# Band attention on TensorE: two heads' products with the keys' low parts side by side, on 64 rows of the array each

## The chip, the cores and the metric

The kernel runs on one core of a Trainium2 chip. Its time is device microseconds (us) for one launch; the median of several runs counts. TensorE (PE) multiplies, VectorE (DVE), ScalarE (ACT) and GpSimd (POOL) work on what comes out, SyncE (SP) issues most DMAs. In this program a TensorE product is a weight load of a stationary tile of up to 128 rows by 128 columns, and then the product itself, which streams a moving tile's columns past it.

## The reference, cut to what matters

The whole is one step of a two-layer encoder: an mLSTM layer and an attention layer, each with a squared-ReLU MLP. The change is in the attention layer: 16 query heads, four for each of 4 key heads, 64 numbers a head, chunks of 64 queries, each of which sees its own chunk and the eight before it.

```python
    def one_chunk(args):
        ci, qb = args
        kb = lax.dynamic_slice_in_dim(kp, ci * CHUNK, span, axis=1)
        vb = lax.dynamic_slice_in_dim(vp, ci * CHUNK, span, axis=1)
        s = jnp.einsum('bqkgd,bskd->bkgqs', qb, kb).astype(jnp.float32) * (HD_B ** -0.5) + bias
        valid = (ci * CHUNK - BAND + jnp.arange(span)) >= 0
        s = jnp.where(valid, s, -jnp.inf)
        p = jax.nn.softmax(s, axis=-1).astype(vb.dtype)
        return jnp.einsum('bkgqs,bskd->bqkgd', p, vb)
```

`span` is 576. There are 16 chunks of the prompt, and a sample of 32 queries, which sees 512 cached keys and its own 32.

## The kernel before, in words

**Numbers in two parts.** Queries and keys are held as a high part (rounded to the format fp32r) and a low part (what the rounding left). A query tile has 128 rows: a head has 64 numbers, and its high part lies in one half of the rows, its low part in the other. Which half holds the high part is set by the head (`hd`, L1712). The keys lie twice: `kk[0]` holds the high part in both halves, `kk[1]` the low part in both halves. So one product with `kk[0]` gives (q high + q low) times k high, and one with `kk[1]` gives (q high + q low) times k low; both are summed in PSUM.

**Units and groups.** A unit is 128 query rows: two heads of one chunk. A group (class `Group`, L1869) is one chunk c and one key head, so two units (`pr` 0 and 1). Two groups (e = 0 and 1) make a pair, whose outputs share one PSUM tile. Chunks 8 to 15 have 576 keys ("wide": each product in two parts of 288 columns); chunks 0 to 7 have 64 to 512 ("slim"). The sample is chunk 16, with one unit in a group. The list `todo` (L1917) runs over two halves of the heads (gp); in each it alternates a wide chunk with a slim one or the sample, 17 pairs, 34 groups. The first two groups (chunk 7) are begun in the stage before.

**A group's way.** `softmax_unit` (L1797): TensorE writes the scores into a PSUM tile `s` (L1804; two buffers of two banks). VectorE adds the bias, scales and takes the minimum in one pass (L1814) into `p`; that frees `s`. ScalarE takes the exponential with its sum (L1817). `normalize`: VectorE's reciprocal (L1823), GpSimd's multiply (L1825). `transposed` (L1827): TensorE turns `p` in blocks of 128 (L1839) into PSUM tiles `pt` (three buffers, each holding four blocks: two key blocks of both units), and ScalarE and VectorE in turn copy them to `pT` (L1848, L1850). `weighted_values` (L1854): for each key block TensorE multiplies the values with both groups' `pT`, one group on 64 columns of the array, the other on the other 64 (L1861, fp32, which the trace records as two products each); ScalarE and VectorE write the result's two parts over the queries (L1866, L1867).

**The order.** The loop at L1986 writes TensorE's order by hand. In step n it is: scores of unit 0 of group n; in odd steps the values of the pair before last; the first four transposes of group n-3; scores of unit 1; the remaining transposes. Every engine works through its own list in order. ScalarE's and VectorE's lists are laid out by the framework from this order (ScalarE's by hand in the first steps alone).

Of the kernel before, what the change touches and what calls it, by code (L numbers as in the profile page):

```python
# [75 lines left out]
def trunk_kernel(ctx: ExitStack, tc: tile.TileContext, a, o):  # L76
# [1610 lines left out]
    for gi, grp in enumerate(((0, 1, 2), (3,))):  # L1687
        ws = {pr: [wblock(f"q{pr}_{half}", wq, 512 * half, 256 * pr) for half in range(2)] for pr in grp}
        for ti, (t0, n) in enumerate(TBS):
            if gi == 0:  # L1690
                flow.finish(norms[ti])
                if ti == 1:
                    flow.finish(norms[2])
                    acc_cm0.__exit__(None, None, None)
                qo_cm.append(tc.tile_pool(name=f"qo{ti}", bufs=1, reuse_waits="tile"))
                QOT.append(qo_cm[ti].__enter__().tile([P, 2, 2, 6 if ti < 2 else 5, 256], F32R, name=f"QO{ti}"))
                if ti == 2:
                    nc.vector.memset(qo(16)[:, :, :, 128:256].bitcast(F32), 0.0)
# [95 lines left out]
    nun, near, groups = [7], {}, {}  # L1794
    bank_n[0] += 6

    def softmax_unit(qst, g, k0, nk, bt, off, mx, nm):  # L1797


        s = bank(f"s_{nm}")[:, None] if near else psT.tile([P, 2, 512], F32, tag="s", name=f"s_{nm}", bufs=2)  # L1800
        parts = [(0, 0, nk)] if nk <= 512 else [(0, 0, nk // 2), (1, nk // 2, nk // 2)]
        for b, j0, w in parts:
            for i in range(2):
                nc.tensor.matmul(s[:, b, :w], qst, kk[i][:, g, k0 + j0:k0 + j0 + w], start=(i == 0), stop=(i == 1))  # L1804
# [64 lines left out]
    class Group:  # L1869


        def __init__(self, gp, c, e):
            self.gp, self.c, self.e, self.g = gp, c, e, 2 * gp + e
            self.nm = f"{gp}_{c}"
            self.mx = at.tile([P, 3, 2], F32, tag="mx", name=f"mx_{self.nm}_{e}", bufs=6)
            self.units = []
            self.n = 2 if c < 16 else 1
            if c < 16:
                self.nk, self.k0 = min(c + 1, 9) * 64, max(0, c - 8) * 64
                self.off = self.k0 % P  # L1880
                self.wid, self.vt0 = self.off + self.nk, (self.k0 - self.off) // P
            else:
                self.nk, self.k0, self.off, self.wid, self.vt0 = 544, TP, 0, 544, 8

        def scores(self, pr):
            if pr >= self.n:
                return
            bt = near[self.e][:, pr] if near else \
                bias[2 * self.g + pr][:, 576 - self.nk:] if self.c < 16 else sbias[self.g]
            self.units.append(softmax_unit(qo(self.c)[:, self.e, self.gp, pr * P:(pr + 1) * P], self.g, self.k0, self.nk,  # L1890
                                           bt, self.off, self.mx[:, :, pr], f"{self.nm}_{self.e}{pr}"))
# [275 lines left out]
```

## Time and profile before

| what | value |
|---|---|
| median of 3 runs | 2409.55 us (2406.93 to 2409.78) |
| the profiled execution's own time | 2412.41 us |
| its span, first to last instruction | 2410.6 us |
| TensorE busy in the span | 2342.7 us, 97% |
| the attention loop | about 1412 to 1601 us of the span |
| granted TensorE clock, mean | 0.995 |

A row of the timeline is start, length, engine, line, operation, tile written and read, array used (rows*columns), moved shape and count; rows of equal neighbours are merged, and a row's length reaches to the end of its last one. Results of a product come out some time after its columns have gone in, so the next row can start before a row ends.

### The profile page before, as it was taken

To read this page: it belongs to the slowest core of one execution; us is meant where nothing else is said; L and a number is where in the kernel's file an instruction comes from. 1 tells how busy PE (TensorE), PEld (TensorE's weight loads), DVE (VectorE), ACT (ScalarE), POOL (GpSimd) and SP (SyncE) were. 2 spreads that over 40 slices of the span, in tenths; PEclk is the share of its full clock that TensorE was granted. 3 is DMA by queue.
4 is the path that set the end of the run, shared out by engine and by line. 5 is a ranking of instruction groups with operands and counts; after the bars stand their busy time and mean duration, and the time that the engine had idled before them with its cause. 6 is when DMAs were issued, how large, how long until landed. Compare 5 with 4: busy or idle time off the path is not lost. (4 is left out here: it accounts for less than half of the span.)

```text
span 2410.6 us, 44188 instructions
## 1 busy us (share of the span) xinstructions
PE 2342.7 (97%) x17180; PEld 2250.4 (93%) x17180; DVE 1939.0 (80%) x3903; ACT 1206.0 (50%) x2454; POOL 168.1 (7%) x320
## 2 busy tenths in 40 slices
PE   7999999999999999999999999999999999899997
PEld 4999999999999999999999987789999999899997
DVE  4888766778788789989888777756998889888778
ACT  4565557278666630101147467773776777222212
POOL 0111100000000000000000224420000000000003
PEclk9999999999999999999999999999999999999999
DMA  8343222526566896675512330051486779976642
GB/s 302 120 131 103 78 89 66 177 91 206 184 198 200 279 336 230 252 261 215 183 56 89 82 93 1 10 140 59 165 278 211 259 278 335 355 256 236 224 146 73
DMA packets 284277, 424.64 MB, mean 176 GB/s; under 512 B 15384, under 2 KB 205228, under 8 KB 278948
## 3 DMA queue, kind: packets, MB, share of 16 engines
q1 hardware_dynamic: 279860, 391.48, 48.3%
q10 hardware_dynamic: 4208, 30.35, 3.1%
q8 instruction: 135, 2.21, 0.4%
q14 instruction: 74, 0.61, 0.1%
HBM read 305.96 MB, written 118.17 MB: 176 GB/s over the span
## 5 line engine op out<-in xcount | busy, mean ns | idle before, releaser
L1082 DVE SCALAR_TENSOR_TENSOR ACX<-dn,ada,ACX 128x264 f32<-128x264 f32 (+6 forms) x664 | 281.8, 447 | 83.2 <-PE dn L1452 41.1
L1452 PE MATMUL dn<-fx,wf_d 128*128 128x264 f32 x2016 | 254.1, 285 | 6.8 <-DVE ACX L1082 3.5
L1452 PEld LDWEIGHTS dn<-fx,wf_d 128*128 128x128 f32 x2016 | 248.8, 188 | 9.0 <-DVE ACX L1082 3.0
L89 ACT CAST w_dn<-raw_dn 128x1024 fp32r<-128x1024 f32 x36 | 37.7, 1050 | 282.1 <-DVE aw L279 136.9
L118 PE MATMUL dn<-hs,w_dn 128*128 128x384 f32 (+2 forms) x512 | 161.2, 315 | 0.0
L119 PE MATMUL dn<-hs,w_dn 128*128 128x384 f32 (+2 forms) x512 | 161.0, 315 | 0.0
L120 PE MATMUL dn<-hs,w_dn 128*128 128x384 f32 (+2 forms) x512 | 156.4, 314 | 1.3 <-DVE w_dn L90 1.3
L1317 PE MATMUL up<-TF,wf_u 128*128 128x264 f32 x1056 | 143.2, 285 | 3.8 <-ACT H L1320 3.8
L1317 PE MATMUL up<-U,wf_u 128*128 128x264 f32 x1056 | 140.3, 285 | 1.7 <-ACT H L1320 1.2
L1317 PE MATMUL up<-u,wf_u 128*128 128x264 f32 x1056 | 139.7, 285 | 1.3 <-ACT wf_u L89 0.7
L279 DVE SCALAR_TENSOR_TENSOR aw<-radw,cs,aw 128x512 f32<-128x512 f32 x196 | 139.5, 743 | 1.1 <-DMA radw<-in_w_ada_dram 1.1
L1317 PEld LDWEIGHTS up<-TF,wf_u 128*128 128x128 f32 x1056 | 134.4, 189 | 4.8 <-ACT H L1320 4.6
L1317 PEld LDWEIGHTS up<-U,wf_u 128*128 128x128 f32 x1056 | 133.0, 188 | 3.0 <-ACT H L1320 1.6
L1317 PEld LDWEIGHTS up<-u,wf_u 128*128 128x128 f32 x1056 | 132.9, 188 | 1.9 <-ACT wf_u L89 0.9
L118 PE MATMUL dn<-U,w_dn 128*128 128x384 f32 (+2 forms) x416 | 129.4, 312 | 0.6 <-DVE ada L304 0.6
L119 PE MATMUL dn<-U,w_dn 128*128 128x384 f32 (+2 forms) x416 | 129.4, 312 | 0.0
L120 PE MATMUL dn<-U,w_dn 128*128 128x384 f32 (+2 forms) x416 | 125.9, 313 | 0.6 <-DVE w_dn L90 0.5
L1817 ACT ACTIVATE p<-p,mx 128x576 f32<-128x576 f32 (+9 forms) x132 | 86.6, 657 | 27.5 <-DVE mx L1814 25.2
L120 PEld LDWEIGHTS dn<-hs,w_dn 128*128 128x128 f32 x512 | 96.0, 188 | 2.0 <-DVE w_dn L90 1.8
L118 PEld LDWEIGHTS dn<-hs,w_dn 128*128 128x128 f32 x512 | 96.5, 189 | 0.1
L119 PEld LDWEIGHTS dn<-hs,w_dn 128*128 128x128 f32 x512 | 96.6, 189 | 0.0
L90 DVE TENSOR_TENSOR HL<-H,HL 128x1056 fp32r<-128x1056 f32 x64 | 80.3, 1254 | 20.0 <-ACT HL L89 19.9
(403 smaller groups left out, 7111.0 us busy)
## 6 DMA issues: line engine op xcount, KB each, us to landing
hpl<-HL SPq DMA_DIRECT2D x144, 264.0 KB
rdn_u<-in_w_up_dram SPq DMA_DIRECT2D x64, 512.0 KB
hd<-HL SPq DMA_DIRECT2D x28, 1056.0 KB
fx<-hd SPq DMA_DIRECT2D x50, 528.0 KB
radw<-in_w_ada_dram SPq DMA_DIRECT2D x24, 1024.0 KB
hd<-HM SPq DMA_DIRECT2D x28, 792.0 KB
raw_up<-in_w_up_dram SPq DMA_DIRECT2D x40, 512.0 KB
raw_dn<-in_w_down_dram SPq DMA_DIRECT2D x36, 512.0 KB
```

The source lines that it names most:

```text
L89: nc.scalar.copy(dst_h, src)
L90: (eng or nc.vector).tensor_sub(dst_l, src, dst_h.bitcast(F32))
L118: nc.tensor.matmul(ps, wh, mov(0, k), start=(k == 0), stop=False)
L119: nc.tensor.matmul(ps, wh, mov(1, k), start=False, stop=False)
L120: nc.tensor.matmul(ps, wl, mov(0, k), start=False, stop=(k == nk - 1))
L279: nc.vector.scalar_tensor_tensor(acc[cnd], raw[:, k], sc, acc[cnd], op0=ALU.mult, op1=ALU.add)
L1082: nc.vector.scalar_tensor_tensor(xs, ps[:, off + o:off + o + mm_], gate[:, fc, cnd:cnd + 1], xs, op0=ALU.mult, op1=ALU.add)
L1317: nc.tensor.matmul(p, self.ws[w][:, wl, k], moving(f, tp, xl, k), start=first and k + n_ == 0, stop=k == 3 and n_ == 2, skip_group_check=n ...
L1452: nc.tensor.matmul(p, ws[w][:, wl, k], t[:, s0, xl], start=first and k + n_ == 0, stop=k == kg - 1 and n_ == 2, skip_group_check=not first)
L1817: nc.scalar.activation(z, z, AF.Exp, bias=mx[:, 0:1], scale=-1.0, accum_out=mx[:, 1:2])
```

## The change

The scores of a group are no longer taken unit by unit. `high` takes unit 0 with the keys' high parts; `low` takes unit 1 with the high parts, and then both units with the low parts: each product reads only the 64 rows that hold that unit's high query part, rows 0 to 63 for unit 0 and 64 to 127 for unit 1, and the two are issued one behind the other. The product of the two low parts is dropped there. So that the high query part lies in the right half, L1712 chooses the half by unit instead of by head. The sample and the first two groups keep full products.

```diff
-                        hi, lo = dst[64 * hd:64 * hd + 64], dst[64 - 64 * hd:128 - 64 * hd]
+                        h0 = 0 if cnd else 64 * (fc % 2)
+                        hi, lo = dst[h0:h0 + 64], dst[64 - h0:128 - h0]
...
+        def key_products(self, pr, i, rows=slice(0, P)):
+
+            if pr == len(self.ss):
+                self.ss.append(score_tile(f"{self.nm}_{self.e}{pr}"))
+            for b, j0, w in key_parts(self.nk):
+                nc.tensor.matmul(self.ss[pr][:, b, :w], qo(self.c)[rows, self.e, self.gp, pr * P:(pr + 1) * P],
+                                 kk[i][rows, self.g, self.k0 + j0:self.k0 + j0 + w], start=(i == 0), stop=(i == 1))
+
+        def high(self):
+            self.key_products(0, 0)
+
+        def low(self):
...
+            if self.n == 1 or near:
+                for pr in range(self.n):
+                    if pr:
+                        self.key_products(pr, 0)
+                    self.key_products(pr, 1)
+                return
+            self.key_products(1, 0)
+            for b, j0, w in key_parts(self.nk):
+                for pr in range(2):
+                    r = slice(64 * pr, 64 * pr + 64)
+                    nc.tensor.matmul(self.ss[pr][:, b, :w], qo(self.c)[r, self.e, self.gp, pr * P:(pr + 1) * P],
+                                     kk[1][r, self.g, self.k0 + j0:self.k0 + j0 + w], start=False, stop=True)
```

The loop's order changes with it. The reductions of both units (`scores`) are now issued behind `low`. In odd steps the order is values, `high`, `low`, all transposes; in even steps four transposes, `high`, the other transposes, `low`.

```diff
-            if new is not None:
+            if n == 4:
                 groups[n] = Group(*todo[n][:3])
-                groups[n].scores(0)
-            if n == 4:
+                groups[n].high()
                 groups[1].values()
             if done and done.e and n > 5:
                 done.values()
...
             turn = old.turn() if old else iter(())
-            next(turn, None)
+            if n % 2 == 0 and n > 5:
+                next(turn, None)
             if new is not None:
-                groups[n].scores(1)
+                if n != 4:
+                    groups[n] = Group(*todo[n][:3])
+                    groups[n].high()
+                if n % 2 == 0 or n < 6:
+                    for _ in turn:
+                        pass
+                groups[n].low()
+                for pr in range(2):
+                    groups[n].scores(pr)
             for _ in turn:
                 pass
```

What that does to TensorE's list, in the first half of the heads, in the step that scores chunk 4 for e = 0 and then takes the values of chunk 5. A name is tile_half_chunk_group-and-unit: `s_0_4_01` is the scores of chunk 4, group e = 0, unit 1; `k0` and `k1` are the keys' high and low parts. Before:

```order
L1804 MATMUL s_0_4_01_16036<-k0_14692,QO0_13787 128x320
L1804 MATMUL s_0_4_01_16036<-k1_14693,QO0_13787 128x320
L1839 MATMUL pt_0_5_1_2_16042<-ident_64,p_0_5_10_15898 128x128
L1839 MATMUL pt_0_5_1_2_16042<-ident_64,p_0_5_11_15925 128x128
L1804 MATMUL s_0_4_10_16047<-k0_14692,QO0_13787 128x320
L1804 MATMUL s_0_4_10_16047<-k1_14693,QO0_13787 128x320
L1861 MATMUL pv_0_5_16053<-pT_0_5_0_16000,V_14694 64x256
L1861 MATMUL pv_0_5_16053<-pT_0_5_1_16029,V_14694 64x256
```

Of the change:

```order
L1892 MATMUL s_0_4_00_16030<-k0_14692,QO0_13787 128x320
L1841 MATMUL pt_0_5_1_2_16032<-ident_64,p_0_5_10_15915 128x128
L1841 MATMUL pt_0_5_1_2_16032<-ident_64,p_0_5_11_15918 128x128
L1892 MATMUL s_0_4_01_16036<-k0_14692,QO0_13787 128x320
L1912 MATMUL s_0_4_00_16030<-k1_14693,QO0_13787 128x320
L1912 MATMUL s_0_4_01_16036<-k1_14693,QO0_13787 128x320
L1863 MATMUL pv_0_5_16046<-pT_0_5_0_16008,V_14694 64x256
L1863 MATMUL pv_0_5_16046<-pT_0_5_1_16022,V_14694 64x256
```

Unit 0's scores were done before the step's last transposes and are now finished by the first of the two 64-row products (L1912); the values follow the 64-row products directly, without the next group's unit 0 between them.

And ScalarE's list around the exponentials of chunk 14, group e = 1 (`p_14_10` and `p_14_11`, units 0 and 1), while chunk 5 is turned (`pT_5_0` and `pT_5_1`, its two groups). Before:

```order
L1817 ACTIVATE p_14_10_15981,mx_14_1_15975<-p_14_10_15981,mx_14_1_15975 128x576
L1866 CAST QO_14296<-pv_13_15984 128x256
L1848 COPY pT_5_0_16000<-pt_5_0_0_16001 128x512
L1817 ACTIVATE p_14_11_16012,mx_14_1_15975<-p_14_11_16012,mx_14_1_15975 128x576
L1848 COPY pT_5_1_16029<-pt_5_1_0_16030 128x512
```

Of the change:

```order
L1868 CAST QO_14296<-pv_13_15975 128x256
L1850 COPY pT_5_0_16008<-pt_5_0_0_16009 128x512
L1819 ACTIVATE p_14_10_16002,mx_14_1_15991<-p_14_10_16002,mx_14_1_15991 128x576
L1819 ACTIVATE p_14_11_16005,mx_14_1_15991<-p_14_11_16005,mx_14_1_15991 128x576
L1850 COPY pT_5_1_16022<-pt_5_1_0_16023 128x512
```

The exponential of unit 0 moved from ahead of the write-out of the values of chunk 13 to behind the copy of `pt_5_0_0`; both exponentials now stand between the two copies.

More of the change, by code (lines that the diff above doesn't have):

```diff
@@ L1795, in trunk_kernel, with key_parts, score_tile, softmax_unit @@
     bank_n[0] += 6
[L1797 to L1804, printed above, removed]
+    def key_parts(nk):
+        return [(0, 0, nk)] if nk <= 512 else [(0, 0, nk // 2), (1, nk // 2, nk // 2)]
+    def score_tile(nm):
+        return bank(f"s_{nm}")[:, None] if near else psT.tile([P, 2, 512], F32, tag="s", name=f"s_{nm}", bufs=2)
+    def softmax_unit(s, nk, bt, off, mx, nm):
+        parts = key_parts(nk)
         nun[0] += 1
@@ L1875, in __init__ @@
             self.mx = at.tile([P, 3, 2], F32, tag="mx", name=f"mx_{self.nm}_{e}", bufs=6)
-            self.units = []
+            self.units, self.ss = [], []
             self.n = 2 if c < 16 else 1
@@ L1889, in scores @@
                 bias[2 * self.g + pr][:, 576 - self.nk:] if self.c < 16 else sbias[self.g]
-            self.units.append(softmax_unit(qo(self.c)[:, self.e, self.gp, pr * P:(pr + 1) * P], self.g, self.k0, self.nk,
-                                           bt, self.off, self.mx[:, :, pr], f"{self.nm}_{self.e}{pr}"))
+            self.units.append(softmax_unit(self.ss[pr], self.nk, bt, self.off, self.mx[:, :, pr],
+                                           f"{self.nm}_{self.e}{pr}"))
         def turn(self):
@@ L2000, in trunk_kernel @@
             turn = old.turn() if old else iter(())
-            next(turn, None)
+            if n % 2 == 0 and n > 5:
+                next(turn, None)
             if new is not None:
-                groups[n].scores(1)
+                if n != 4:
+                    groups[n] = Group(*todo[n][:3])
+                    groups[n].high()
+                if n % 2 == 0 or n < 6:
+                    for _ in turn:
+                        pass
+                groups[n].low()
+                for pr in range(2):
+                    groups[n].scores(pr)
             for _ in turn:
```

## The prediction

> **What bounds the kernel now.** I read the page first, for who is busy and how the profiled execution stands to its span.
>
> ```profile
> span 2410.6 us, 44188 instructions
> PE 2342.7 (97%) x17180; PEld 2250.4 (93%) x17180; DVE 1939.0 (80%) x3903; ACT 1206.0 (50%) x2454; POOL 168.1 (7%) x320
> ```
>
> TensorE is the bound over the whole; the execution took 2412.41 us, 1.81 more than its span, and 2.86 more than the median of the runs. That does not say what bounds the attention loop. For that, the windows view over the loop, then its groups by shape.
>
> ```profile
> 1412.30:1601.00 188.70, 183.66 (x1416) 141.54 (x1417) 135.68 (x448) 140.68 (x379) 82.48 (x160) 1.00 0.10 25
> L1861 PE MATMUL pv<-pT,V 128*64 128x256 f32 x416 | 54.6, 387 | 0.5 <-DVE mx L1814 0.3 <-ACT pT L1848 0.2
> L1804 PE MATMUL s<-k,QO 128*128 128x288 f32 x256 | 49.6, 317 | 1.1 <-ACT ks L1963 0.6 <-DVE mx L1814 0.4
> ```
>
> Of 188.7 us TensorE is busy 183.7, ScalarE 140.7, VectorE 135.7: TensorE leads here too, but the others have only a quarter to spare, and each works its list in order. Whether they can follow is a matter of sequence, so I read the timeline of three engines where the wide chunk 14 meets the slim chunks 5 and 4. TensorE:
>
> ```profile
> 1443.15 0.60 PE L1804 MATMUL s<-k,QO 128*128 128x384 f32 x2
> ...
> 1444.15 0.78 PE L1804 MATMUL s<-k,QO 128*128 128x288 f32 x4
> 1444.78 0.60 PE L1839 MATMUL pt<-ident,p 128*128 128x128 f32 x4
> 1445.13 0.78 PE L1804 MATMUL s<-k,QO 128*128 128x288 f32 x4
> 1445.74 0.82 PE L1839 MATMUL pt<-ident,p 128*128 128x128 f32 x6
> 1446.32 0.78 PE L1804 MATMUL s<-k,QO 128*128 128x288 f32 x4
> 1447.02 2.38 PE L1861 MATMUL pv<-pT,V 128*64 128x256 f32 x20
> 1449.33 0.66 PE L1839 MATMUL pt<-ident,p 128*128 128x128 f32 x4
> 1449.75 0.78 PE L1804 MATMUL s<-k,QO 128*128 128x288 f32 x4
> ...
> 1452.62 1.65 PE L1861 MATMUL pv<-pT,V 128*64 128x256 f32 x12
> 1454.20 0.66 PE L1839 MATMUL pt<-ident,p 128*128 128x128 f32 x4
> 1454.61 0.55 PE L1804 MATMUL s<-k,QO 128*128 128x320 f32 x2
> ```
>
> From end to end of the last scores of a pair, the wide pair took 6.78 (1443.75 to 1450.53), the slim one 4.63 (to 1455.16). Slots come from differences: six transposes ahead of scores take 0.58 from start to start, four take 0.35, so a transpose has a slot of 0.11; the 2.17 between the scores at 1444.15 and 1446.32 hold ten of them and eight products of 288 columns, so such a product has 0.13. A row's length adds some 0.17 that the next work overlaps.
>
> **What the change removes.** Where a group had four slots for each key part it has three: two units high, and one that both units' low products share. A wide group loses 2 x 0.133. The 256 products of 288 columns are 32 wide groups: 8.5 us. Thirty slim groups lose one slot each, 0.20 for 448 columns down to 0.11, about 0.145 in the mean: 4.3. Together -12.8, if two 64-row products do run side by side. No row shows that for halves of the rows. The nearest row is the values', on halves of the columns: of 20 records the last starts 2.00 after the first (2.38 less the mean 0.387), so 0.10 each, less than the 0.12 that 256 columns need at the scores' rate. So I take one slot for two; the other end is two slots, no gain at all.
> [...]
>
> **What it adds on the array.** Narrower products change how the array is divided. What a change of division costs:
>
> ```profile
> 1427.97 2.53 PE L1861 MATMUL pv<-pT,V 128*64 128x256 f32 x20
> 1430.43 0.65 PE L1839 MATMUL pt<-ident,p 128*128 128x128 f32 x4
> ```
>
> ```profile
> 45.81 0.28 PE L487 MATMUL v<-w_v,U 128*128 128x264 f32 x1
> 45.93 0.28 PE L488 MATMUL v<-w_v,U 128*128 128x264 f32 x1
> 46.14 0.24 PE L344 MATMUL tp_p<-ident,rows 28*128 28x28 f32 x1
> ```
>
> ```profile
> 1505.13 0.40 PE L1804 MATMUL s<-k,QO 128*128 128x288 f32 x1 [0.20 <-DVE mx L1814]
> ```
>
> Going to 28 rows, the next start is 0.21 away instead of 0.12: 0.09 is lost. Chunk 13's values (only blocks of 128 keys) take 2.31 to the next transpose; chunk 12's (1427.97), whose last block has 64 keys, take 2.46: 0.15 for changing rows alone, 0.10 idle and 0.05 because the first product then waits for its own weights, 64 columns of them. With 128 columns that wait is 0.10: a first product after a pause takes 0.40, where one in the stream takes about 0.30. Leaving the values costs the same way, 0.31 instead of 0.216 to the next start, and the first four transposes take 0.66 instead of 0.60.
> So for a pair of groups: going in, twice 0.09 + 0.10; coming out to transposes in the odd step, 0.10 + 0.06 (the even step goes out to the values, and that change was paid before too); and the values are now followed by a score product, not a transpose, 0.05 more. Sum 0.59, for 31 pairs (16 wide, 15 slim) 18.4 us. Against -12.8 that is +5.6 on TensorE alone. The bounds are 0 and twice that; I take the rows, since two different changes agree.
> [...]
>
> **What it moves.** This decides. Both reductions now wait for the group's end, and ScalarE's list changed as the order shows. ScalarE and VectorE before:
>
> ```profile
> 1446.66 0.56 ACT L1848 COPY pT<-pt 128x512 f32<-128x512 f32 x1
> 1447.22 0.78 ACT L1817 ACTIVATE p<-p,mx 128x576 f32<-128x576 f32 x1
> ...
> 1450.08 0.58 ACT L1848 COPY pT<-pt 128x512 f32<-128x512 f32 x1 [0.23 <-PE pt L1839]
> 1451.36 0.78 ACT L1817 ACTIVATE p<-p,mx 128x576 f32<-128x576 f32 x1 [0.70 <-DVE mx L1814]
> 1452.05 0.19 ACT L1817 ACTIVATION_READ_ACCUMULATOR p<-p,mx 128x1 f32 x1
> 1452.14 0.56 ACT L1848 COPY pT<-pt 128x512 f32<-128x512 f32 x1
> 1452.61 0.56 ACT L1817 ACTIVATE p<-p,mx 128x320 f32<-128x320 f32 x1
> ```
>
> ```profile
> 1450.56 0.76 DVE L1814 CUSTOM_DVE_ANT_0 p<-s,bias 128x576 f32<-128x576 f32 x1 [0.26 <-PE s L1804]
> 1451.24 0.08 DVE L1814 DVE_READ_ACCUMULATOR2_ANT mx<- 128x1 f32 x1
> ```
>
> Before, the copy that the values of chunk 5 need (1452.14) came after one exponential, and TensorE hardly waited. Now count from the end of chunk 14's last scores.
> Slim part: chunk 5's transposes begin at about -0.07 (0.30 of a product's length, less its slot 0.13, less 0.10 for leaving). Four end at 0.59; the copy starts 0.09 later (1449.99 to 1450.08), at 0.68; the exponential 0.56 later, 1.24; the second 2.02; the copy of `pt_5_1_0` 2.80; it ends at 3.36, and the values start at 3.4. TensorE meanwhile has twelve transposes, unit 0 high, then unit 1 high, which waits for the second reduction (0.03 + 2 x 0.68 + 0.08, about 1.5), then the pair: ready at 2.1. It waits 1.3. Then six value slots (1.35), 0.10 out, two high products and 0.10 (0.40), 0.09 in, the pair to its end (0.40): 5.75 instead of 4.63, +1.1.
> Wide part, counted anew: ten transposes to 1.1; the next four need the first `pt` buffer, whose copy runs 0.68 to 1.24: 1.3 to 1.73; unit 0 high 2.0; four more 2.44; the last two need the third buffer, whose copy stands behind the two slim exponentials (1.24 + 2 x 0.56 + about 0.37 = 2.73): to 2.97; unit 1 high 3.25; the pair 3.8; the values 2.46; high products 0.63; the pair to its end 0.6: 7.5. Chunk 14's values, like chunk 12's, hold the extra 0.15, which the 6.78 lacks: +0.6.
> Both include the array's costs. Fourteen wide pairs (the first two are in the loop's opening steps) give 14 x 0.6 = 8.4. The slim wait is full where the late copy stands behind both wide exponentials: chunks 5, 4 and 2 in the first half, 7, 5, 4 and 2 in the second, 7 x 1.1 = 7.7. For 6, 3 and the sample, VectorE has the other group's first copy, or the late one is needed late: six times about 0.3, 1.8. Sum +18, so 2430.4 for the profiled execution and 2427.5 for the median.
> The other edits are nothing: the query parts' halves change place, not size, in a stage of which TensorE's list is unchanged; the reciprocals and GpSimd's multiplies are needed three steps later. Were that cover gone, transposes would wait for GpSimd. No DMA moves.
>
> **The rivals.** *The array alone.* ScalarE has 25% to spare; if it catches up, TensorE's +5.6 is left: 2415 for the median. For it: before, TensorE seldom waited. Against: the wait is one of order, not of load. Chance 0.15.
> *Faster.* If 64-row products follow full ones without a break, 12.8 goes, and what waits remain take back some third: 2409.55 - 8 = 2401. It decides once a change of division costs under 0.4 for a pair of groups instead of 0.59 and the copies are in time. For it: no row has this very division, 64 rows by 128 columns. Against: 28 rows by 128 columns and 64 by 64 both paid. Chance 0.10. [...]
> *The pairs run one behind the other.* Then the change does not do what it says: 94 further slots of 0.11 to 0.13 are 10 to 12.5, of which the slim waits hide about a third: 2435. Chance 0.13.
>
> **How the numbers follow.** The forecast has 0.62. The range reaches down past the array-alone case to 2411 (half of the moves' cost is my hand-made schedule, uncertain by 0.4 in each part) and up to 2438 for serial pairs. A measurement can tell about 0.2% from no change, 4.8 us: below 2404.7 is faster, above 2414.4 slower. Faster has 0.10 and a little, 0.12; the low edge of the array-alone case gives 0.08 for the same; slower 0.80.
>
> **What would show it.** Right: in the timeline after, two L1912 products start within about 0.01 of each other; some 0.09 is lost before them; the values of chunks 5, 4 and 2 wait 1 us or more for ScalarE's `pT` copy; the loop takes about 207 us, with ScalarE no busier. Wrong: TensorE's waits in the loop stay near 5 us, or pairs start a full slot apart.

## The result, and the profile after

The changed kernel takes 2435.9 us (median of 4 runs, 2433.71 to 2438.7), beside 2409.66 for the kernel before (4 runs, 2406.93 to 2411.81): +26.2 us, a ratio of 1.0111 (95% interval 1.0095 to 1.0127). The profiled execution took 2438.70 us, 2.1 more than its span. The head of its page:

```profile
span 2436.6 us, 44167 instructions
PE 2355.4 (97%) x17180; PEld 2241.1 (92%) x17180; DVE 1944.3 (80%) x3903; ACT 1203.5 (49%) x2454; POOL 167.3 (7%) x320
```

ScalarE has no more work than before and VectorE hardly more; TensorE has as many products, but 12.7 us more busy time. The windows view over the attention loop, cut at the same two instructions as before (there 188.70 long):

```profile
1407.47:1625.79 218.32, 199.79 (x1416) 135.17 (x1417) 140.22 (x448) 135.99 (x379) 82.96 (x160) 0.98 0.09 22
```

The loop takes 29.6 us more, in which TensorE stands idle for 18.5 us instead of 5.0; ScalarE worked 136.0 us of it, before 140.7. TensorE's busy time grew by the other 16.1 us. That is not more work: a record is some 0.17 us longer than its slot (0.30 beside 0.13 for 288 columns in the profile before), so a product that starts late by less than that leaves no idle time, and its lateness counts as busy; and where the granted clock was 0.50 the records were longer (0.51 in the mean for 288 columns on full rows from 1411.49 to 1421.73, 0.33 from 1430 to 1600). The granted clock is 0.98 in place of 1.00, of which more below. (The stages ahead were 4.8 us shorter than in the profile before and those behind 1.2 longer. In every other trace of this study, whatever it changes, the last scores of the first pair end 1.7 to 5.5 us earlier than in that one profile, so this belongs to that execution and not to the change.) Where TensorE waits, the groups by shape tell; the transposes before, then three groups after:

```profile
L1839 PE MATMUL pt<-ident,p 128*128 128x128 f32 x432 | 67.1, 277 | 1.0 <-DVE k L1741 0.6 <-ACT pT L1848 0.4
```

```profile
L1841 PE MATMUL pt<-ident,p 128*128 128x128 f32 x432 | 63.9, 281 | 8.6 <-ACT pT L1850 7.1 <-DVE k L1742 1.4
L1863 PE MATMUL pv<-pT,V 128*64 128x256 f32 x416 | 57.9, 397 | 3.6 <-ACT pT L1850 3.4
L1892 PE MATMUL s<-k,QO 128*128 128x288 f32 x128 | 31.1, 342 | 3.8 <-DVE mx L1816 3.1 <-ACT ks L1995 0.6
```

Transposes and values wait for ScalarE's copies `pT`, as forecast; the same transposes waited 0.4 before. The timeline of TensorE at the place that the prediction worked out, chunk 14 between the slim chunks 5 and 4:

```profile
1448.28 0.51 PE L1892 MATMUL s<-k,QO 128*128 128x288 f32 x2
1448.72 0.54 PE L1912 MATMUL s<-k,QO 64*128 64x288 f32 x4
1449.19 2.38 PE L1863 MATMUL pv<-pT,V 128*64 128x256 f32 x20
...
1454.74 0.41 PE L1912 MATMUL s<-k,QO 64*128 64x320 f32 x2
1455.08 0.65 PE L1863 MATMUL pv<-pT,V 128*64 128x256 f32 x2
1456.07 1.51 PE L1863 MATMUL pv<-pT,V 128*64 128x256 f32 x10 [0.34 <-ACT pT L1850]
```

ScalarE there:

```profile
1453.43 0.59 ACT L1850 COPY pT<-pt 128x512 f32<-128x512 f32 x1 [1.34 <-PE pt L1841]
1453.91 0.78 ACT L1819 ACTIVATE p<-p,mx 128x576 f32<-128x576 f32 x1
...
1454.68 0.77 ACT L1819 ACTIVATE p<-p,mx 128x576 f32<-128x576 f32 x1
...
1455.44 0.57 ACT L1850 COPY pT<-pt 128x512 f32<-128x512 f32 x1
```

The first product of chunk 5's values (two records) runs; the other five (ten records) need the copy that stands behind both exponentials of chunk 14's second group. It starts at 1455.44 and ends at 1456.01, and they start at 1456.07: 0.99 after the first, where a product takes some 0.20.

Where the 29 us lie, pair by pair, comes from the timelines: from the end of one pair's last score product to the end of the next pair's, after less before. The opening (chunks 8, 12 and 6 of the first half): +5.2. Ten wide pairs with a slim neighbour on both sides (chunks 10, 11, 13, 14, 15, twice): +8.7. Ten slim pairs (chunks 2 to 5 of the first half, 2 to 7 of the second): +6.8. Chunks 1 and 0, at the end of each half: +4.8. The other six (the two samples, chunk 9 twice, and 8 and 12 of the second half): +3.7. The same count is made for the experiments, below.

### The profile page after: what moved, and what is told of

It is laid out like the page before. It is cut to its first block, busy times and chain, and to the rows that moved or that the text cites. A ratio compares the mean times of both kernels' runs of the same rounds, so it can differ in the third digit from the quotient of the medians.

```text
span 2436.6 us, 44167 instructions
## 1 busy us (share of the span) xinstructions
PE 2355.4 (97%) x17180; PEld 2241.1 (92%) x17180; DVE 1944.3 (80%) x3903; ACT 1203.5 (49%) x2454; POOL 167.3 (7%) x320
## 4 chain that ended last, share of the span: by engine, by line
PE 63%; DVE 19%; ACT 7%; DMA 5%; issue 3%; POOL 0%; SPq 0%; DVEq 0%; ACTq 0%; POOLq 0%
PE dn L1452 11%; PE up L1317 9%; PE dn L120 5%; PE dn L119 5%; PE dn L118 5%; PE pv L1863 2%; DVE wf_u L90 2%; PE pt L1841 2%; PE up L120 2%; PE up L119 2%; PE up L118 2%; PE op_b L118 1%; PE op_b L119 1%; PE op_b L120 1%; PE s L1892 1%
## 5 line engine op out<-in xcount | busy, mean ns | idle before, releaser
L90 DVE TENSOR_TENSOR HL<-H,HL 128x1056 fp32r<-128x1056 f32 x64 | 80.2, 1253 | 18.6 <-ACT HL L89 18.4
```

Of the source, the lines that this page charges most:

```text
L90: (eng or nc.vector).tensor_sub(dst_l, src, dst_h.bitcast(F32))
```

## The experiments

Each was timed beside the kernel before on the same chip; differences are between the two medians. The half-widths of the intervals are 2.3 to 5.9 us, so that a step of 2 us between two kernels is read from the traces or not at all. The last five columns are the count by pairs in each kernel's one trace.

| kernel | over the kernel before, us | ratio (95% interval) | opening | 10 wide | 10 slim | 4 last | 6 other |
|---|---|---|---|---|---|---|---|
| changed | 26.2 | 1.0111 (1.0095 to 1.0127) | 5.2 | 8.7 | 6.8 | 4.8 | 3.7 |
| 1 same rows | 38.7 | 1.0157 (1.0143 to 1.0171) | 2.2 | 13.3 | 9.8 | 5.2 | 5.4 |
| 2 division alone | 26.3 | 1.0105 (1.0091 to 1.0118) | 0.7 | 12.2 | 7.6 | 2.2 | 4.1 |
| 3 order alone | 24.2 | 1.0099 (1.0085 to 1.0113) | 1.0 | 8.7 | 4.5 | 4.5 | 3.6 |
| 4 opening as before | 23.7 | 1.0094 (1.0079 to 1.0110) | -0.1 | 8.7 | 6.8 | 4.8 | 3.7 |
| 5 exponential later | 18.6 | 1.0075 (1.0063 to 1.0088) | 1.2 | 7.1 | 3.8 | 2.3 | 3.4 |
| 6 transposes spread | 27.4 | 1.0108 (1.0093 to 1.0124) | 1.7 | 6.1 | 8.4 | 2.3 | 3.2 |
| 7 spread, exponential later | 21.3 | 1.0082 (1.0068 to 1.0096) | 4.0 | 3.9 | 6.0 | 3.5 | 5.1 |
| 8 full, unit by unit | 24.1 | 1.0098 (1.0084 to 1.0112) | 3.7 | 9.2 | 3.1 | 4.5 | 2.8 |
| 9 full, late but spread | 23.0 | 1.0089 (1.0065 to 1.0114) | 4.1 | 6.1 | 6.8 | 1.6 | 3.3 |
| 10 full, unit by unit and spread | 6.6 | 1.0026 (1.0016 to 1.0035) | 1.4 | 1.4 | 0.2 | 1.1 | 0.6 |
| 11 as 8, exponential later | 12.6 | 1.0060 (1.0046 to 1.0075) | 1.0 | 9.1 | 0.4 | 1.6 | 2.1 |
| 12 parts that helped | 15.4 | 1.0066 (1.0053 to 1.0078) | -0.3 | 7.8 | 2.6 | 1.9 | 2.9 |

Two things disturb the columns. Kernel 6's profiled execution was 4.8 us under its median, and kernel 7's 3.9 over its own. And the granted clock fell to 0.50 inside the loop of two traces: in kernel 1 from 1580.04 for 3.4 us, in kernel 7 from 1517.07 for 6.8 and from 1609.23 for 3.4. The slim pair of chunk 4 that the first one met lost 2.6, in the changed kernel 0.9, so kernel 1's 9.8 holds some 1.7 of it; those of kernel 7 lie in its last two columns.

### What the array does: kernels 1 and 2

Kernel 1 puts both units' low products on the same 64 rows, to keep them from sharing a slot. Unit 1 then multiplies its low query part, which lies in rows 0 to 63, where its high part belongs.

```diff
-                    r = slice(64 * pr, 64 * pr + 64)
+                    r = slice(0, 64)
```

> The changed kernel, but both units' low products use rows 0 to 63, so that they cannot run side by side; unit 1's low product is then made of its high parts, everything else is the same. It prices the sharing of slots. My theory: the starts of a pair move from 3 to 4 ns apart to a slot of 0.11 to 0.13; 94 pairs of groups' products, twice for the wide chunks (about 154 slots): some 18 us on TensorE, of which waits that are there anyway hide a third or more: 8 to 14 us over the changed kernel. Rival 'the waits set the time, the slots are free': under 3 us over the changed kernel.

Measured: 38.7 over the kernel before, 12.5 over the changed one. (The expectation counted the wide groups' pairs twice over: 94 already has two for each wide group, so 94 slots of about 0.13, some 12 us, is what it should have said. It also called the wrong part unit 1's high one.) The 12.5 lie within the 8 to 14 expected, uncertain by some 5. In the traces, outside the opening and without the fall of the clock, some 8 are lost, 4.6 of them in the ten wide pairs: 0.46 each, where four slots are 0.53. The rows show a slot each. The first group of chunk 14, from unit 1's high products to the values, in kernel 1 and then with full products (kernel 9), to be set beside 1448.28 to 1449.19 above:

```profile
1447.81 0.52 PE L1892 MATMUL s<-k,QO 128*128 128x288 f32 x2
1448.25 0.79 PE L1912 MATMUL s<-k,QO 64*128 64x288 f32 x4
1448.97 2.38 PE L1863 MATMUL pv<-pT,V 128*64 128x256 f32 x20
```

```profile
1446.29 0.51 PE L1892 MATMUL s<-k,QO 128*128 128x288 f32 x2
1446.63 0.69 PE L1912 MATMUL s<-k,QO 128*128 128x288 f32 x4
1447.26 2.38 PE L1863 MATMUL pv<-pT,V 128*64 128x256 f32 x20
```

1.16 on the same rows, 0.91 in pairs, 0.97 in full. Pairs save two slots of 0.13 against the same rows: they do run side by side. Against full products they save 0.06 only, since the first pair starts 0.44 after the first high product and not 0.34, and then needs another 0.1 for its own weights: its weight load starts with it, at 1448.72, where the second high product's starts 0.13 ahead (1448.37 to 1448.50), and its records are 0.40 long, those of the second pair 0.30.

Kernel 2 has the order of the kernel before, and each unit's low product alone on its own 64 rows, behind its high products; the half of the high query part is chosen by unit, as in the changed kernel.

```diff
-        for b, j0, w in parts:
-            for i in range(2):
-                nc.tensor.matmul(s[:, b, :w], qst, kk[i][:, g, k0 + j0:k0 + j0 + w], start=(i == 0), stop=(i == 1))
+        for i in range(2):
+            rows = r if i else slice(0, P)
+            for b, j0, w in parts:
+                nc.tensor.matmul(s[:, b, :w], qst[rows], kk[i][rows, g, k0 + j0:k0 + j0 + w], start=(i == 0),
+                                 stop=(i == 1))
...
+                                           slice(64 * pr, 64 * pr + 64) if self.n == 2 and not near else slice(0, P)))
```

> The order of the kernel before is kept; each unit's low product runs on its own 64 rows, alone, right behind its high products, so no slot is freed and the array's division changes twice for each of 124 units. By the prediction's prices: 124 x 0.19 going in, 93 x 0.16 coming out to transposes: 38 us over the kernel before, less what falls into waits that were there. Rival 'a change of division costs next to nothing' (then the freed slots should have shown, and the order ate them): within 5 us of the kernel before.

Measured: 26.3. A change of division is far from free. By the prediction's prices a wide pair should lose 4 x 0.19 + 3 x 0.16 = 1.24; the ten wide pairs lost 12.2, 1.22 each. The prices hold there. The 38 did not come, since slim pairs lost 0.76 each and the opening 0.7. Of the 12 that are missing some 4 are idle time that is gone: from the end of the first pair's scores to the end of the last one's TensorE stood still for 5.1 us before and 1.3 here (for VectorE's `mx` its products waited 2.8, here 0.4). Where the rest went no row shows. One unit of that kernel, two high and two low products; before, four full ones took 0.63 from start to start (1444.15 to 1444.78):

```profile
1450.77 0.97 PE L1806 MATMUL s<-k,QO 128*128 128x288 f32 x4
1451.67 0.44 PE L1842 MATMUL pt<-ident,p 128*128 128x128 f32 x2
```

It takes 0.90 (1450.77 to 1451.67), 0.27 more; the prices for going in and for the idle time of coming out are 0.19 and 0.10.

### What the order does: kernel 3

The changed kernel's order with full products.

```diff
-                    r = slice(64 * pr, 64 * pr + 64)
+                    r = slice(0, P)
```

> The new order of the loop is kept, but both units' low products use all 128 rows again, so they follow one another: no shared slot, and no change of the array's division at the scores. My theory (the price lies in the order: both exponentials of a wide group now stand on ScalarE between the two late copies, and both reductions wait for the group's end): it stays slow, 20 to 24 us over the kernel before, 3 to 6 under the changed one (the array's net 5.6 goes, part of it only turns into waiting), and the values of chunk 5's second group still wait 0.3 us or more for ScalarE's pT copy. Rival 'the array alone' (the slowdown is the changes of division): at most 5 us over the kernel before, what the opening steps lose.

Measured: 24.2. So the order alone makes nearly all of the loss, and the rival that it is the array falls. It is 2.0 under the changed kernel, less than expected and within the intervals; chunk 5's values still stand 0.37 us for ScalarE's copy (at 1454.07 of its trace). In wide pairs the narrow products make no difference that the trace shows (8.7 in both kernels); slim pairs pay 2.3 of the difference.

### The opening: kernel 4

The changed kernel with the first two wide pairs in the order and with the full products of the kernel before.

```diff
+            if n < 6:
+                groups[n] = Group(*todo[n][:3])
+                groups[n].unit(0)
             if n == 4:
-                groups[n] = Group(*todo[n][:3])
-                groups[n].high()
                 groups[1].values()
...
+            if n < 6:
+                groups[n].unit(1)
```

> The changed kernel, but its opening steps (the first two wide pairs of groups) have the order and the full products of the kernel before. In the changed kernel's profiled run these steps took 5.2 us longer, with the granted clock at 0.50 for 10.2 us. If the new order opened the waits that let the clock fall: about 5 us under the changed kernel, 21 over the one before, and a clock of 1.00 between the last key product and the loop. Rival (the clock fell by chance in that one run, or falls for a reason ahead of these steps): same time as the changed kernel within 2 us, with the fall still there or in neither.

Measured: 23.7, 2.5 under the changed kernel, half of the 5 expected and within what the intervals allow for no difference; but the trace is plain. The opening's 5.2 is gone (-0.1), the clock does not fall, and all else is the same to 0.1. What those steps looked like after the change, in the windows view (the column ahead of the last two is the granted clock), and before:

```profile
1408.00:1412.00 4.00, 1.84 (x15) 1.24 (x13) 2.40 (x9) 1.04 (x4) 0.00 (x0) 0.94 1.06 253
1412.00:1416.00 4.00, 3.81 (x16) 3.18 (x16) 2.14 (x8) 2.21 (x5) 0.43 (x1) 0.50 1.00 247
1416.00:1420.00 4.00, 3.21 (x14) 1.98 (x16) 1.58 (x5) 1.63 (x4) 2.35 (x4) 0.50 0.78 174
1420.00:1424.00 4.00, 3.04 (x17) 1.66 (x14) 1.86 (x5) 1.01 (x2) 0.16 (x1) 0.78 0.00 0
```

```profile
1412.00:1416.00 4.00, 2.95 (x20) 2.52 (x21) 3.88 (x12) 1.85 (x7) 0.00 (x0) 1.00 1.06 252
1416.00:1420.00 4.00, 3.82 (x26) 2.62 (x25) 2.16 (x8) 3.41 (x9) 0.00 (x0) 1.00 1.04 252
```

With less to do while it waits for the keys, TensorE was busy for 1.84 of 4 us; then its granted clock was 0.50 for 10.2 us, and sixteen products kept it busy for 3.81 us where before 26 took 3.82. It does not happen each time. Of the ten profiles with the new opening four have the fall there (the changed kernel and kernels 7, 8 and 9), and their openings cost 3.7 to 5.2; the six without it cost 1.0 to 2.2, 1.4 in the mean. None of the four profiles with the old opening (before, and kernels 2, 4 and 12) has it.

### The exponentials' place: kernel 5

TensorE's list stays; on ScalarE the second unit's exponential of an odd step is issued behind the next step's first copies.

```diff
             if n % 2 == 0 and n > 5:
                 next(turn, None)
+                if groups.get(n - 1):
+                    groups[n - 1].exps(1)
```

> The changed kernel with TensorE's list untouched; only on ScalarE the second unit's exponential of every odd step is issued behind the next step's first copies, so that one and not both exponentials stand ahead of the copy for which the values wait. My theory (the price is the place of those exponentials): each slim part gains up to 0.78 of its 1.0, each wide part 0.3 to 0.5 of its 0.6 to 0.9: 8 to 14 us under the changed kernel, 12 to 18 over the one before. Rival 'the array alone': no change from the changed kernel within 2 us. Rival 'the late reductions': TensorE then waits for VectorE's mx where it waited for pT; a gain under 4 us.

Measured: 18.6, so 7.6 under the changed kernel, just short of the 8 to 14. In the table the slim pairs win 3.0, the last pairs 2.5, the wide ones 1.6, in all 7.4 outside the opening (and the opening, in this trace without the fall of the clock, 4.0). The mechanism is there, at about half the size that the upper end gave it; both rivals fall. The edit issues the normalizing behind the moved exponential too, and TensorE's transposes now wait 2.4 us for GpSimd, where they waited for none before, so a part of the gain is lost again.

### The transposes' place: kernels 6 and 7

In the changed kernel's odd steps ten transposes come in a row, where before no more than six did. A new theory was that this bunching is the rest of the loss.

```diff
                     groups[n].high()
+                if n % 2 and n > 5:
+                    next(turn, None)
                 if n % 2 == 0 or n < 6:
```

> The changed kernel with one move on TensorE: in odd steps the first four transposes stand between the two units' high products again, so no more than six follow one another where ten did; the number of changes of division stays. In the trace of the changed kernel the gaps from one transpose to the next are 0.145 in the mean, before 0.115, and TensorE waits some 10 us for a pt buffer still to be copied, before 0.4. Theory 'bunched transposes' (three pt buffers, a copy takes longer than four transposes): these gaps fall back, 4 to 8 us under the changed kernel, 18 to 22 over the one before. Rival 'late reductions': unit 1's reduction and both exponentials now start another 0.46 later in each of 30 odd steps, and TensorE waits for these: no gain, or up to 6 us over the changed kernel.

> The same move, on top of the kernel in which the second unit's exponential of odd steps is issued behind the next step's first copies (2428.2). There TensorE still waits 3.8 us and more for ScalarE's pT copies between transposes. Bunched transposes: 3 to 7 us less than that kernel, 2421 to 2425, if both causes stand side by side. Rival: the two edits take away the same wait, and this comes out within 1.5 us of the better of the two.

Measured: 27.4 and 21.3, no gain in either case by the medians. The theory fell as it stood, and the table shows why: the wide pairs won 2.6 and 3.2, and the slim ones lost 1.7 and 2.2 (in kernel 6's trace 3.9 are won outside the opening, with the last pairs' 2.5). In kernel 6 transposes wait 0.2 us instead of 6.3 for ScalarE's copies, but 3.0 instead of 0.4 for VectorE's, and scores 4.9 instead of 2.5 for VectorE's reductions, which the spread pushes back. That suggested that two chains lie side by side, and that breaking either is enough.

### Two chains: kernels 8 to 11

These have full products throughout, so that the array has no part in it. Kernel 3 is the corner "late and bunched". Kernel 8 takes unit 0 whole where its high product stood (its reduction and exponential too), and leaves the transposes bunched. Kernel 9 is kernel 6 in full: late, but spread. Kernel 10 has both put right.

```diff
+            if n > 5 and new is not None:
+                groups[n] = Group(*todo[n][:3])
+                groups[n].unit(0)
+                if n % 2:
+                    next(turn, None)
+                else:
+                    for _ in turn:
+                        pass
+                groups[n].unit(1)
```

This is kernel 10 against kernel 3 (`unit` is a unit's high and low products and then its `scores`); kernel 8 is without the `next` in odd steps.

> The kernel with the new order and full products (24.2 us over the one before), with one thing put back from step 6 on: unit 0's low products follow its high ones at once, and its reduction and exponential are issued there, instead of at the group's end. The transposes stay where the new order has them, the values too. Theory 'late reductions' (two score tiles; nothing of a group is reduced until its pair is through): the larger part of what the order costs goes, 8 to 14 us less, 10 to 16 over the kernel before. Rival 'place of the transposes and of the exponentials behind them': it stays within 3 us of the 24.2.

> As the run above, and in odd steps the first four transposes stand between the units again: what is left of the new order is that the values come one unit earlier and the even steps' transposes all ahead of unit 1. Late reductions: little more to gain, 0 to 4 us under the run above, 8 to 14 over the kernel before. Rival: only here does the time fall, to within 5 us of the kernel before. Both at work: some 5 us under the run above.

> Full products throughout, so the array has no part in it: both units' low products and reductions stay at the group's end, but in odd steps the first four transposes stand between the units. It is the fourth corner: late and bunched 24.2 us over the kernel before, early and bunched 24.1, early and spread 6.6. Theory 'two chains that cover each other' (whichever is broken, the reductions' or the transposes', TensorE stands still as long): late and spread costs as much as either, 20 to 26 us, with TensorE waiting for VectorE's mx and hardly for pT. Rival 'the transposes' place is all, and only the narrow pairs spoiled it in the kernel with pairs': 6 to 12 us over the kernel before.

Measured: 24.1, 6.6 and 23.0. By these medians early reductions alone give 0.1, spread transposes alone 1.2, both 17.6. The traces say much the same: outside the opening, where the clock did not fall in these four, kernel 3 loses 21.3, kernel 8 19.6, kernel 9 17.7 and kernel 10 3.2. What the wait is in each corner, from the waits of TensorE between 1425 and 1617 us (total, times, longest): kernel 8, where the transposes are bunched,

```profile
PE pt L1841 <- ACT pT L1850: 10.0, 17, 1.6
PE pv L1863 <- ACT pT L1850: 5.4, 7, 1.6
PE s L1892 <- DVE mx L1816: 0.8, 2, 0.4
```

and kernel 9, where the reductions are late:

```profile
PE s L1892 <- DVE mx L1816: 5.4, 17, 0.6
PE pt L1841 <- DVE pT L1852: 2.8, 8, 0.5
PE pv L1863 <- ACT pT L1850: 1.2, 4, 0.6
```

The wait changes its name. In kernel 9 it is also shorter, 10.1 us in all against 16.2, though the time is nearly the same; the rest of its loss does not show as idle time. But kernel 10's ScalarE list is not that of kernel 8: where the transposes are spread, the framework by itself puts the late copy ahead of the second exponential. Kernel 11 keeps TensorE's list of kernel 8 and issues that exponential of a wide group later by hand, which gives ScalarE's order of kernel 10 around the wide groups' exponentials.

```diff
-                groups[n].unit(1)
+                groups[n].unit(1, n % 2 == 0)
+                if n % 2:
+                    next(turn, None)
+                    groups[n].exps(0)
+                    if groups[n].nk <= 512 or groups[n].n < 2:
+                        groups[n].exps(1)
...
             if n % 2 == 0 and n > 5:
                 next(turn, None)
+                if n > 6 and groups.get(n - 1) and groups[n - 1].nk > 512 and groups[n - 1].n == 2:
+                    groups[n - 1].exps(1)
```

> TensorE's list is that of the run with units early and transposes bunched (24.1 us over the kernel before). Only on ScalarE the second unit's exponential of odd steps is issued behind the next copies, which is about the list that came by itself where the transposes were spread as well (6.6). It splits those 17.5 us: theory 'the exponentials' place is the cause, the transposes' place only sets it': 6 to 10 us over the kernel before. Theory 'the transposes' own place costs too': ScalarE's part is what it was in the kernel with pairs, 6 to 9 us, and 15 to 18 over the kernel before stay. Rival 'neither alone': 21 or more.

Measured: 12.6, between the first two expectations (the ratio beside it, 1.0060, would make it 14.5): of the 17.5, the exponentials' place is 11.5 and what is left to kernel 10 is 6.0, each uncertain by some 4 to 5, and kernel 8's opening has the fall of the clock in it. The traces divide them more cleanly, and otherwise: outside the opening kernel 8 loses 19.6, kernel 11 13.2 and kernel 10 3.2, so 6.4 and 10.0. From kernel 8 to 11 the slim pairs go from 3.1 to 0.4 and the last ones from 4.5 to 1.6, while the wide ones stay at 9.1. From 11 to 10 the wide ones go from 9.1 to 1.4, and the slim ones stay. The timelines of both engines show the two. The slim part, chunk 14 to chunk 4, in kernel 8 and then in kernel 11:

```profile
1453.48 0.78 ACT L1819 ACTIVATE p<-p,mx 128x576 f32<-128x576 f32 x1
...
1454.26 0.76 ACT L1819 ACTIVATE p<-p,mx 128x576 f32<-128x576 f32 x1
1454.31 0.65 PE L1863 MATMUL pv<-pT,V 128*64 128x256 f32 x2
1455.02 0.57 ACT L1850 COPY pT<-pt 128x512 f32<-128x512 f32 x1
...
1455.64 1.51 PE L1863 MATMUL pv<-pT,V 128*64 128x256 f32 x10 [0.68 <-ACT pT L1850]
```

```profile
1448.76 0.78 ACT L1925 ACTIVATE p<-p,mx 128x576 f32<-128x576 f32 x1
...
1449.53 0.57 ACT L1849 COPY pT<-pt 128x512 f32<-128x512 f32 x1
1449.58 2.09 PE L1862 MATMUL pv<-pT,V 128*64 128x256 f32 x12
1450.00 0.78 ACT L1925 ACTIVATE p<-p,mx 128x576 f32<-128x576 f32 x1
```

From the first value product to the end of the last it is 2.84 in the one (1454.31 to 1457.15) and 2.09 in the other, one exponential less. The wide part, where chunk 5's second group is followed by chunk 14's first, in kernel 8 and then in kernel 10:

```profile
1444.67 1.25 PE L1841 MATMUL pt<-ident,p 128*128 128x128 f32 x10
1445.24 0.62 ACT L1819 ACTIVATE p<-p,mx 128x384 f32<-128x384 f32 x1 [0.85 <-DVE mx L1816]
1445.85 0.56 ACT L1850 COPY pT<-pt 128x512 f32<-128x512 f32 x1
...
1446.56 0.63 PE L1841 MATMUL pt<-ident,p 128*128 128x128 f32 x4 [0.63 <-ACT pT L1850]
```

```profile
1442.58 0.60 PE L1841 MATMUL pt<-ident,p 128*128 128x128 f32 x4
1442.93 0.59 PE L1892 MATMUL s<-k,QO 128*128 128x384 f32 x2
1443.27 0.59 ACT L1850 COPY pT<-pt 128x512 f32<-128x512 f32 x1 [0.63 <-PE pt L1841]
1443.37 1.27 PE L1841 MATMUL pt<-ident,p 128*128 128x128 f32 x10
1443.75 0.62 ACT L1819 ACTIVATE p<-p,mx 128x384 f32<-128x384 f32 x1
```

In kernel 8 the first four transposes are through at about 1445.3 (1444.67, three slots of 0.11 and a length of 0.28) and their copy starts at 1445.85, since the slim exponential stands ahead of it; ten transposes have filled the `pt` buffers and TensorE stops for 0.63. With four transposes between the units the copy comes first, and ten run without a stop. Kernel 11 has not changed that: there too the slim exponential stands ahead of the copy, and TensorE stops as long.

```profile
1440.51 0.62 ACT L1925 ACTIVATE p<-p,mx 128x384 f32<-128x384 f32 x1 [0.85 <-DVE mx L1816]
1441.13 0.56 ACT L1849 COPY pT<-pt 128x512 f32<-128x512 f32 x1
1441.84 0.63 PE L1840 MATMUL pt<-ident,p 128*128 128x128 f32 x4 [0.63 <-ACT pT L1849]
```

So kernel 10 differs from kernel 11 in two things at once, the transposes' place and, in this part, ScalarE's order. The 7.7 of the wide pairs belong to both together; a kernel with bunched transposes and the copy ahead of the slim exponential is not among these.

### The parts that helped: kernel 12

Kernel 5 with the opening of kernel 4, and with slim groups unit by unit on all rows.

```diff
+                slim = groups[n].nk <= 512 or groups[n].n == 1
+                if slim:
+                    groups[n].unit(0, n % 2 == 0)
+                else:
                     groups[n].high()
```

> The parts that helped, together: pairs only in the wide groups (a slim group goes unit by unit on all rows), the opening steps of the kernel before, and the second unit's exponential of odd steps behind the next copies. From 18.6 over the kernel before: 2.5 for the opening, 2.9 for the slim groups' changes of division (the difference of the slim parts between the changed kernel and the one with full products), 3 to 6 for their reductions: 7 to 11 us over the kernel before. Rival 'the parts take away the same waits': 13 or more. No version here is expected under the kernel before, since a wide pair of groups frees 0.53 and pays 0.59.

Measured: 15.4, the rival's case: the edits take away the same waits in part. Its ten wide pairs still cost 7.8. No kernel here is faster than the kernel before; the nearest, kernel 10, is 6.6 over it, holds no narrow product, and differs from the kernel before in the opening, and in that the values come a unit earlier and the even steps' transposes all stand ahead of unit 1.

## Why the prediction was right, and where not

The sign and the range held (2411 to 2438); the 2427.5 was 8.4 too low. Step by step:

**Freed slots, 12.8.** Right. In the trace the two starts of a pair lie 3 or 4 ns apart in 79 of the 94 pairs, and in none more than 10 ns, and giving the slots back costs 12.5 (kernel 1, uncertain by some 5). The rival "one behind the other" falls with this.

**Changes of division, 18.4.** The price was right, 1.22 for a wide pair of kernel 2 against 1.24. By the same prices the change costs a wide pair 0.06 net and a slim one 0.30, together the prediction's +5.6. Between kernel 3 and the changed one there are 2.0; in the traces 2.3 in the ten slim pairs, priced 3.0, and none in the ten wide, priced 0.6. Where the rest went no row shows. The rival "the array alone" falls with kernel 3, "faster" with kernels 1 and 2 together: freed slots and lost ones nearly cancel, as forecast.

**The moves, +18.** The step that decided was right in kind and short in two terms. Where it was worked out by hand, it met the trace: the part from chunk 14 to chunk 4 took 5.66 (forecast 5.75), the wide part 7.44 (forecast 7.5). Over all, the ten wide pairs lost 0.87 each (forecast 0.6), while the seven slim pairs lost 0.64 (forecast 1.1); the wait of chunk 5's values is 0.8 instead of 1.3. That these two errors nearly cancel is luck. What failed are two terms that the sum left at nothing without a reason, the opening steps and the last pairs of each half (chunks 1 and 0): 5.2 and 4.8, so 10 us that it did not have. The opening lost some 1.4 to the order and, in four of ten profiles, 2.3 to 3.8 more with the fall of the clock; the last pairs lost theirs to the exponentials' place as well, since moving one takes 2.9 of 4.5 off them (kernel 11 against 8). That they have so few transposes to cover it is likely the reason, which was not tried.

**"ScalarE's list" as the cause.** Shown, but not alone. Moving one exponential took 7.6 off the changed kernel and 11.5 off kernel 8; in the traces, outside the opening, 7.4 and 6.4. The prediction saw the `pt` buffers in the wide part and put their wait down to the same list. Kernel 10, with the transposes spread, takes away 7.7 of kernel 11's 9.1 us there; since its copy also moved ahead of the slim exponential, it stays open whether the transposes' place costs of itself or through ScalarE's list, as forecast. What the prediction did not see is that there are two chains: late reductions without bunched transposes cost 23.0, bunched transposes without late reductions 24.1, both 24.2.

**The wrong-if conditions.** Neither came: TensorE's idle time in the loop went from 5.0 to 18.5, and the pairs start together. Of the signs for being right two came in part alone. The values were to wait 1 us or more for the late copy in every such part; they stood still for ScalarE's copies four times, 2.8 us in all. And the forecast loop of about 207 us was 218.3, by the two terms above and the larger wide parts.

**Left open.** What decides whether the clock falls in the opening: kernels 5 and 11 had TensorE busy for only 1.93 and 1.85 of the same 4 us, without the fall. It is open too whether bunched transposes cost anything once the copy stands ahead of the slim exponential. Nor was it tried whether more score tiles would let the pairs keep their order.

## What to carry to other kernels

Before two products are put side by side, count what must wait for both of them: here two wide groups freed 0.53 us and, by the prices that kernel 2 bears out, paid 0.59 on the array at once, while the consumers, which had been fed one unit at a time, got two units in a lump and queued up behind each other. On an engine that takes its list in order, as ScalarE did here (the copy at 1455.44 stood behind two exponentials of 0.78 and 0.77), cost a reordering by writing out the list of the engine that copies for the bottleneck, and look for the short copy that now stands behind long work; and when undoing one suspected cause changes next to nothing, undo two, since parallel chains hide each other. Steps at the start and the end of a loop deserve their own line in the sum: here, priced at zero, they made 10 of the trace's 29 us.

## What the hardware showed

A fall of the granted clock far outlasted the lull of TensorE ahead of it: in the changed kernel's trace, after 2.2 us of idle time in 4, the granted clock was 0.50 for 10.2 us; in kernels 7, 8 and 9 it was so for 6.8. Those four openings cost 2.3 to 3.8 us more than the mean of the six without a fall. The lull alone does not decide: in the 4 us from 1408, towards the end of which the clock fell in the changed kernel and in kernels 7 and 8 (mean 0.94, 0.91 and 0.95), TensorE was busy for 1.84, 1.96 and 1.92, and in kernels 1, 5 and 11, where it did not fall, for 1.93, 1.93 and 1.85. What else it takes was not shown.

A change between full rows and 64 rows cost much the same whether the narrow product stood alone or in a pair. In the pair at 1448.72 of the changed kernel the first start is 0.44 behind the first high product, in kernel 9's full products 0.34: 0.10 going in. Its records are 0.40 long beside 0.30 for the second pair's, another 0.10; and the values start 0.47 behind it, of which two slots of 0.13 and those 0.10 leave 0.10 for coming out. Alone, the 4 ways in and 3 out of kernel 2's wide pair come to 1.22 us, where the prediction's prices, 0.19 in and 0.16 out, give 1.24.
